# Second FFN by seven block products: the output product by token halves, one half's operands first, four column blocks together

## The chip, the cores and the metric

The kernel runs on one core of one Trainium2 chip. The core has five engines that run side by side and wait for each other by semaphores: TensorE (PE, matrix products into the accumulator memory PSUM), VectorE (DVE), ScalarE (ACT), GpSimd (POOL) and SyncE (SP, which here issues the DMA transfers, one after the other from one queue). The metric is the device time of one execution in microseconds (us), the median over the runs.

## The reference

A decoder trunk of two layers on 1024 tokens of width 1024 in float32. Layer 0 is a Conformer convolution, layer 1 an attention with forget gates; behind each stands an FFN of inner width 4096 and a gated per-layer embedding. The change touches the end of layer 1's attention and layer 1's FFN:

```python
h = h + o @ attn_w_o                       # the attention's output product
hn = rmsnorm(h, ffn_norm[i])               # per token: divided by its root mean square
h = h + jnp.square(jax.nn.relu(hn @ ffn_w1[i])) @ ffn_w2[i]
```

## The kernel before

Activations are kept transposed: features on the 128 partitions, tokens along the free axis, in two halves of 512 tokens (h = 0, 1). A tile hTb0 or hTb1 is one half of the residual, 8 panels of 128 features. A matrix product in the precision wanted takes three matmuls: each operand is split into a high half (a cast to fp32r on ScalarE, line 111) and a low half (the value less its high half, a subtraction on VectorE or GpSimd, line 112), and high by high, low by high and high by low are added in PSUM. Each matmul is 128 x 128 by 128 x 512.

**Attention output product** (`out_product`, L770 to L776; accumulators ps_wo, weights wo). It is done in two parts along the inner dimension: panels 0 to 4 for half 0, then for half 1, then panels 5 to 7 for both halves by turns. Each result is added to hTb on VectorE.

**Operands of the FFN** (`tokens`, L420). For each half the statistics: squares on ScalarE (sq_f), summed on VectorE (acc_f), a small matmul set with a column of 1/1024 (st_f), a mean (ms_f, VectorE), a power of -1/2 (r_f, GpSimd), a broadcast by matmul (bc_f) and its copy (bs_f, ScalarE). f10 is half 0's, f11 half 1's. Then the normed activations, in blocks of 4 panels (z1, z2; L428 is the norm: scale, gain and broadcast in one instruction for a panel), their differences (L439), and of the seven operand blocks the high and low halves (xf).

**The FFN** (`ffn_both`) takes both matrix products by blocks: tokens in two halves, inner features in two halves, columns in two halves, so that seven block products do the work of eight, at the price of sums and differences of blocks. The products are numbered 1 to 7; `seven` runs them in the order 1, 5, 6, 3, 7, 2, 4. Products 1, 6, 7 and 4 accumulate in one bank per output (chain 0), 5, 3 and 2 in another (chain 1). A bank that goes on from one product to the next is first read out. The weight blocks of a product are made in `weight`: for products 5, 6 and 3 the tile t (wt in the first matrix, wu in the second) is built up by a sum or difference on VectorE (L408, L410, L412), for 7 a raw block is overwritten (L414).

- First matrix (`ffn_in`, accumulators psa, raw weights rwa, split weights wa): eight groups of two column blocks, 2 x 12 matmuls per product. Evacuations e, relu and square (L527) and the differences (L532) make the operands of the second matrix's seven products, which go to DRAM (rd).
- Second matrix (`ffn_out`, accumulators psb, rwb and wb): four column groups c of four outputs, 48 matmuls per product. Operands are loaded from DRAM (rb) and split again (rx). The results are added to the residual, which was put by in DRAM (hd) and comes back as hTc0 and hTc1. The raw weights of a group are two tiles of 2 MB; three such buffers exist.

The order on each engine is that in which the program is written, but for statistics, whose matmuls get a higher priority in a scheduling pass; the transfers on SyncE's queue are issued in that order too, each as soon as what it waits for is done.

## Time and profile before

| | us |
|---|---|
| median of 3 runs | 2645.2 |
| lowest and highest | 2643.66, 2648.96 |
| the profiled execution | 2649.79 |
| its span | 2648.1 |
| TensorE busy in the span | 2460.8 |
| VectorE busy | 1794.9 |
| ScalarE busy | 1066.6 |
| GpSimd busy | 938.1 |

The span runs from the first to the last instruction in the trace of one execution; the rest of an execution's time lies around it. TensorE is busy for 93% of it, so what matters is where it is not, and what it waits for there. The slices of the page are 66 us wide; the views below go to the two places by their times.

### The profile page before, as it was taken

The page shows a single profiled execution, that of the slowest core. Times are in us where ns is not written, and L with a number is a line of the kernel's source. Part 1 is how long each engine was busy: PE and PEld are TensorE (multiplying, and loading weights), DVE is VectorE, ACT ScalarE, POOL GpSimd, SP SyncE. Part 2 cuts the span into 40 slices and gives each one's busy share as a digit, 9 for nine tenths or more (in the row PEclk, how much of TensorE's full clock was granted, in tenths as well). Part 3 has the DMA queues.
Part 4 walks back from the last instruction along what each step waited for, and adds up shares of the span by engine and source line. Part 5 has one row for each costly group of instructions (what it writes and reads, how often), then busy time and mean ns, then how long its engine had stood idle before and what let it go on. Part 6 is the DMA issues. An engine that isn't in the chain of part 4 may idle for free.

```text
span 2648.1 us, 31325 instructions
## 1 busy us (share of the span) xinstructions
PE 2460.8 (93%) x11672; PEld 2055.2 (78%) x11672; DVE 1794.9 (68%) x2719; ACT 1066.6 (40%) x1646; POOL 938.1 (35%) x759
## 2 busy tenths in 40 slices
PE   7996899999999999989999999797699995999996
PEld 6885778888888888868888887586588884888875
DVE  7999999525644346565677776756856657777765
ACT  5245433223433225334565665633333233343442
POOL 3464534444000000013666665611632223454400
PEclk9998899999999999989999999898899997999997
DMA  3124123333323333222111111332234455443133
GB/s 130 48 77 170 62 82 98 101 97 96 95 90 101 96 96 100 96 106 68 55 43 54 43 64 57 104 106 93 91 134 157 175 190 208 159 159 127 52 123 112
DMA packets 92008, 272.37 MB, mean 103 GB/s; under 512 B 9280, under 2 KB 14016, under 8 KB 89808
## 3 DMA queue, kind: packets, MB, share of 16 engines
q1 hardware_dynamic: 90704, 266.17, 29.6%
q10 hardware_dynamic: 1152, 4.19, 0.4%
q8 instruction: 92, 1.51, 0.2%
q14 instruction: 60, 0.49, 0.1%
HBM read 216.26 MB, written 54.07 MB: 102 GB/s over the span
## 4 chain that ended last, share of the span: by engine, by line
PE 77%; DVE 13%; ACT 3%; issue 2%; POOL 2%; DMA 2%; SPq 0%; DVEq 0%; POOLq 0%; ACTq 0%
PE ps_fb L137 13%; PE ps_fa L137 12%; PE psb L137 10%; PE psa L137 10%; PE ps_gt L137 6%; PE psq L137 3%; DVE ya L332 3%; PE psv L137 3%; PE psk L137 3%; PE pg L137 3%; PE ps_wo L137 3%; PE pa L137 3%; PE po L946 2%; PE t L976 2%; PE ps_pw L137 2%
## 5 line engine op out<-in xcount | busy, mean ns | idle before, releaser
L137 PE MATMUL psa<-xf,wa 128*128 128x512 f32 x1344 | 315.3, 397 | 21.3 <-ACT wa L111 13.6
L137 PE MATMUL psb<-rx,wb 128*128 128x512 f32 x1344 | 307.7, 391 | 27.2 <-ACT wb L111 26.9
L137 PEld LDWEIGHTS psa<-xf,wa 128*128 128x128 f32 x1344 | 257.7, 192 | 78.5 <-ACT wa L111 14.5
L137 PEld LDWEIGHTS psb<-rx,wb 128*128 128x128 f32 x1344 | 253.8, 189 | 81.2 <-ACT wb L111 27.3
L332 DVE SCALAR_TENSOR_TENSOR ya<-u,wdw,ya 128x512 f32<-128x512 f32 x420 | 284.0, 745 | 0.0
L111 ACT CAST wh_fb<-raw_fb 128x1024 fp32r<-128x1024 f32 x64 | 67.2, 1053 | 213.9 <-PE ps_fb L137 134.7
L111 ACT CAST wh_fa<-raw_fa 128x1024 fp32r<-128x1024 f32 x64 | 67.4, 1053 | 206.4 <-PE ps_fa L137 110.6
L390 DVE TENSOR_TENSOR hT<-ps_fb,hT 128x512 f32<-128x512 f32 x64 | 44.1, 688 | 147.8 <-PE ps_fb L137 147.8
L205 POOL TENSOR_TENSOR r_g<-ms_g,mhalf 128x4 f32<-128x4 f32 x4 | 5.3, 1326 | 375.8 <-DVE ms_g L203 375.8
L928 POOL TENSOR_SCALAR pr<-pr,sm 128x896 f32<-128x896 f32 (+7 forms) x128 | 98.1, 768 | 100.3 <-DVE sm L927 94.1
L112 DVE TENSOR_TENSOR pt<-t,pt 128x512 fp32r<-128x512 f32 (+1 forms) x160 | 99.1, 633 | 49.9 <-ACT pt L111 48.8
L946 PE MATMUL po<-pt,V 128*128 128x256 f32 x640 | 122.2, 307 | 9.5 <-ACT pt L111 7.5
L112 POOL TENSOR_TENSOR wb<-rwb,wb 128x1024 fp32r<-128x1024 f32 x32 | 81.8, 2556 | 122.4 <-ACT wb L111 122.4
L112 DVE TENSOR_TENSOR rx<-rb,rx 128x1024 fp32r<-128x1024 f32 x56 | 92.2, 1654 | 48.6 <-ACT rx L111 48.5
L926 ACT ACTIVATE pr<-pr,sm 128x896 f32<-128x896 f32 (+7 forms) x128 | 99.3, 776 | 51.6 <-DVE sm L925 34.8
L906 POOL TENSOR_SCALAR pr<-cb,ctok 128x896 f32<-128x896 f32 (+7 forms) x128 | 105.4, 829 | 38.9 <-PE t L976 31.2
L920 DVE CUSTOM_DVE_ANT_0 pr<-s,pr 128x512 f32<-128x512 f32 (+2 forms) x192 | 103.4, 550 | 22.5 <-POOL pr L907 11.7
L384 DVE SCALAR_TENSOR_TENSOR fa<-ps_fa,bs_f 128x512 f32<-128x512 f32 x64 | 43.8, 689 | 108.7 <-PE ps_fa L137 105.2
L111 ACT CAST pt<-t 128x512 fp32r<-128x512 f32 (+1 forms) x160 | 83.9, 539 | 76.3 <-PE t L976 73.1
L112 POOL TENSOR_TENSOR wl_fb<-raw_fb,wh_fb 128x1024 fp32r<-128x1024 f32 x32 | 77.3, 2419 | 104.6 <-ACT wh_fb L111 104.6
L112 POOL TENSOR_TENSOR wl_fa<-raw_fa,wh_fa 128x1024 fp32r<-128x1024 f32 x32 | 79.1, 2471 | 91.0 <-ACT wh_fa L111 90.9
L976 PE MATMUL t<-ident,pr 128*128 128x128 f32 x576 | 97.5, 280 | 11.2 <-POOL pr L928 6.0
(355 smaller groups left out, 7043.9 us busy)
## 6 DMA issues: line engine op xcount, KB each, us to landing
raw_fa<-in_wf SPq DMA_DIRECT2D x64, 512.0 KB, 3.4
raw_fb<-in_wf SPq DMA_DIRECT2D x64, 512.0 KB, 3.5
rd<-e SPq DMA_DIRECT2D x112, 256.0 KB, 3.5
rb<-rd SPq DMA_DIRECT2D x28, 1024.0 KB, 5.3
rwa<-in_wf SPq DMA_DIRECT2D x32, 512.0 KB, 5.8
rwb<-in_wf2s SPq DMA_DIRECT2D x8, 2048.0 KB, 9.7
raw_gt<-in_wgate SPq DMA_DIRECT2D x24, 512.0 KB, 3.6
proj<-pj SPq DMA_DIRECT2D x32, 256.0 KB, 2.4
```

The lines of the kernel that those rows point to most:

```text
L111: copy(h, src)
L112: sub.tensor_tensor(l, src, h.bitcast(F32), ALU.subtract)
L137: self.nc.tensor.matmul(ps, p[:, k, :], q[:, k, :], start=(start and k == k0 and n == 0), stop=(stop and k == kt - 1 and n == 2), skip_gro ...
L332: nc.vector.scalar_tensor_tensor(d, s(j), w(j), o, ALU.mult, ALU.add)
L384: nc.vector.scalar_tensor_tensor(t, ps, 0.0, s[h][1], ALU.max, ALU.mult)
L390: nc.vector.tensor_tensor(hT[h][:, j, :], ps, hT[h][:, j, :], ALU.add)
L906: nc.gpsimd.tensor_scalar(z, cb[:, 0:W], -1.0, self.ctok[:, i, n : n + 1], ALU.mult, ALU.add)
L920: nc.vector.tensor_tensor_reduce(zz, ps[:, 0 : hi - lo], zz, -1.0, 3.0e38, ALU.add, ALU.min, sm[:, m : m + 1])
L926: nc.scalar.activation(z, z, AF.Exp, bias=sm[:, 0:1], scale=-1.0, accum_out=sm[:, 2:3])
L928: nc.gpsimd.tensor_scalar(z, z, sm[:, 3:4], 1.0, ALU.mult, ALU.mult)
L946: nc.tensor.matmul(po, V[:, j, n % 4, :], pt[:, q, c : c + 256], start=(j == 0 and q == 0), stop=(jp == u and jj == 1 and q == 1),)
L976: nc.tensor.transpose(ps[:, c : c + P], pr[b][:, j * P : (j + 1) * P], self.ident)
```

## The change

- The attention's output product is done for half 0 to its end (panels 0 to 4, 5 to 7), then for half 1. Behind half 0 stands `tokens_first`: half 0's statistics and the operands 1 and 2, which need half 0 alone. The rest of half 1's product is written behind that.
- `tokens_rest` (half 1's statistics and operands 5, 6, 3, 7, 4) is written behind product 1 and product 2 of the first matrix. The low halves of all operands are subtracted on VectorE, not on GpSimd. Operand 2 is stored to DRAM and loaded again for the later groups (x2b).
- The first call of `ffn_in` takes groups 0 and 1 together: four outputs, 48 matmuls per product. The products run in the order 1, 2, 5, 6, 3, 7, 4 (but in the last column group of the second matrix, which keeps the old order), and product 2 accumulates in a chain of its own.
- Raw weights are tiles of 512 KB, one per block (and pair of outputs), in pools of 4 (wr, used by both matrices) and 8 (wq), loaded one by one; the second matrix's array is laid out anew for that. The blocks of the second matrix's operands are loaded into the place of their low half.
- Product 4's result is put through relu and square on ScalarE.

```diff
-    def tokens(self, hT, gain, name):
-        hd = self.dr.tile([NH, P, KT * HB], F32, name=f"hd_{name}")
-        bc = [self.stats(hT, h, name)[1] for h in range(NH)]
...
-            for q in range(2):
-                s = slice(2 * q, 2 * q + 2)
-                self.split(src[:, s], x[p][:, 0, s], x[p][:, 1, s], sub=nc.gpsimd)
...
+    def parts(self, src, xh, xl, sub=None):
+        for q in range(2):
+            s = slice(2 * q, 2 * q + 2)
+            self.split(src[:, s], xh[:, s], xl[:, s], sub=sub)
+        return xh, xl
+    def tokens_first(self, hT, gain, name):
+        hd = self.dr.tile([NH, P, KT * HB], F32, name=f"hd_{name}")
+        self.nc.sync.dma_start(hd[0], hT[0].rearrange("p k t -> p (k t)"))
+        bc = self.stats(hT, 0, name)[1]
+        f = self.slot([P, 2, 4, HB], F32, f"z0{name}")
+        x = {}
+        for p, i in ((1, 0), (2, 1)):
+            self.norm4(f[:, i], hT[0], gain, 4 * i, bc)
+            t = self.block(f"x{name}{p}")
+            x[p] = self.parts(f[:, i], t[:, 0], t[:, 1])
+        return hT, x, f, hd, gain, name
+    def tokens_rest(self, hT, x, f, hd, gain, name):
+        nc.sync.dma_start(hd[1], hT[1].rearrange("p k t -> p (k t)"))
+        xd = self.dr.tile([P, 2, 4, HB], F32, name=f"xd_{name}")
+        bc = self.stats(hT, 1, name)[1]
+        g = self.slot([P, 2, 4, HB], F32, f"z1{name}")
...
+        def later():
+            nc.sync.dma_start(xd[:, 0], x[2][0].bitcast(F32))
+            nc.sync.dma_start(xd[:, 1], x[2][1].bitcast(F32))
+            self.norm4(g[:, 1], hT[1], gain, 4, bc)
+            self.diff(f[:, 0], g[:, 1], f[:, 0])
+            new(6, f[:, 0])
+            new(3, g[:, 1])
+            self.diff(g[:, 0], g[:, 1], g[:, 0])
+            self.diff(f[:, 1], f[:, 1], f[:, 0])
+            new(7, g[:, 0])
+            new(4, f[:, 1])
+            t = self.block(f"x{name}2b")
+            nc.sync.dma_start(t.bitcast(F32), xd)
+            x[2] = (t[:, 0], t[:, 1])
+        self.norm4(g[:, 0], hT[1], gain, 0, bc)
+        self.diff(f[:, 0], g[:, 0], f[:, 0])
+        new(5, f[:, 0])
+        return later
-    def seven(self, w, x, n, k4, name, banks, done):
+    def seven(self, w, x, n, k4, name, done, order=(1, 2, 5, 6, 3, 7, 4), between=None):
-        for p in (1, 5, 6, 3, 7, 2, 4):
+        for p in order:
-            chain = {1: 0, 6: 0, 7: 0, 4: 0, 5: 1, 3: 1, 2: 1}[p]
+            chain = {1: 0, 6: 0, 7: 0, 4: 0, 5: 1, 3: 1, 2: 2}[p]
...
+            if between:
+                between(p)
...
-                for g in range(8):
...
-                    self.ffn_in(l, g, raw, sp, x, rd)
+                load(0)
+                load(1)
+                rest = []
+                def between(p):
+                    if p == 1:
+                        rest.append(self.tokens_rest(*first))
+                    elif p == 2:
+                        rest[0]()
+                self.ffn_in(l, (0, 1), raw, sp, x, rd, between)
+                for g in range(2, 8):
+                    load(g)
+                    self.ffn_in(l, (g,), raw, sp, x, rd)
...
-                wr = self.pool(c2, f"wq{l}", 3)
+                wq = self.pool(c2, f"wq{l}", 8)
...
-            if p == 4:
                 o = tt(p)
-                nc.scalar.copy(o, ps)
-                square(o, o)
-                keep(2, i, o)
...
+                nc.scalar.activation(o, ps, AF.Relu)
+                nc.scalar.activation(o, o, AF.Square)
+                keep(2, o)
...
+        for b in range(4):
+            for q in range(2):
+                pool, tag = (wq, "wq") if b > 1 else (wr, "wr")
+                raw = pool.tile([P, 2, HB], F32, name=f"rwb{l}{c}{b}{q}", tag=tag)
+                nc.sync.dma_start(raw, self.a["wf2s"][l, c, q, :, b].rearrange("p (n f) -> p n f", n=2))
+                raws[q].append(raw)
...
+        order = (1, 5, 6, 3, 7, 2, 4) if c == 3 else (1, 2, 5, 6, 3, 7, 4)
+        self.seven(w, x, 4, 4, f"b{l}{c}", done, order)
...
-            for h in range(NH):
-                for _ in self.out_product(0, KSPLIT, (h,), self.at):
+            for k0, k1, h in ((0, KSPLIT, 0), (KSPLIT, NP, 0), (0, KSPLIT, 1)):
+                for _ in self.out_product(k0, k1, (h,), self.at):
...
+            first = self.tokens_first(self.hn, "ffn1", "f1")
+            for _ in self.out_product(KSPLIT, NP, (1,)):
                 pass
-        return self.hn
+        return first
```

TensorE at joint 1, between the output product and the products of the first matrix. psa10_ij names group 0's accumulators: the first of the three digits is the chain, the second the product that began it, the third the output; xf1p is the operand of product p, wa10p and wa11p are the weights of groups 0 and 1. Before:

```order
L137 MATMUL ps_wo571_15059<-xoh1_13676,wl_wo570_15045 128x512
L189 MATMUL st_f10_15088<-meanm_75,acc_f10_15089 128x1 x4
L158 MATMUL bc_f10_15120<-ident_68,r_f10_15118 128x128 x4
L189 MATMUL st_f11_15127<-meanm_75,acc_f11_15128 128x1 x4
L158 MATMUL bc_f11_15159<-ident_68,r_f11_15157 128x128 x4
L137 MATMUL psa10_010_15235<-xf11_15171,wa101_15236 128x512 x12
L137 MATMUL psa10_011_15253<-xf11_15171,wa101_15236 128x512 x12
L137 MATMUL psa10_150_15268<-xf15_15182,wa105_15270 128x512
```

Both sets of statistics stand ahead of the first product. In the changed kernel:

```order
L137 MATMUL psa10_012_15243<-xf11_15028,wa111_15244 128x512 x10
L137 MATMUL psa10_013_15261<-xf11_15028,wa111_15244 128x512 x10
L189 MATMUL st_f11_15278<-meanm_75,acc_f11_15279 128x1 x4
L158 MATMUL bc_f11_15310<-ident_68,r_f11_15308 128x128 x4
L137 MATMUL psa10_220_15329<-xf12_15037,wa102_15330 128x512 x12
L137 MATMUL psa10_221_15348<-xf12_15037,wa102_15330 128x512 x12
L137 MATMUL psa10_222_15364<-xf12_15037,wa112_15365 128x512 x12
L137 MATMUL psa10_223_15383<-xf12_15037,wa112_15365 128x512 x12
L137 MATMUL psa10_150_15433<-xf15_15324,wa105_15435 128x512
L137 MATMUL psa10_151_15452<-xf15_15324,wa105_15435 128x512
```

Half 0's statistics have gone from here (they stand among the matmuls of the output product), and half 1's stand between product 1 (operand xf11) and product 2 (xf12), which now has two pairs of outputs.

VectorE at the same place in the changed kernel, from the last sums of half 1's squares (acc_f11) to the low half of the operand of product 5 (xf15); wt10 is group 0's weight sum, e101 and e111 are results of products 1 and 2:

```order
L197 TENSOR_TENSOR acc_f11_15279<-acc_f11_15279,sq_f11_6_15296 128x512
L197 TENSOR_TENSOR acc_f11_15279<-acc_f11_15279,sq_f11_7_15299 128x512
L409 TENSOR_TENSOR wt10_15208<-wt10_15208,rwa100_15195 128x1024
L203 TENSOR_SCALAR ms_f11_15306<-st_f11_15278 128x4
L422 SCALAR_TENSOR_TENSOR z1f1_15317<-hTb1_13907,vec_66,bs_f11_15315 128x512 x8
L436 TENSOR_TENSOR z0f1_15023<-z1f1_15317,z0f1_15023 128x1024 x2
L582 TENSOR_TENSOR e101_15226<-psa10_220_15329,e101_15226 128x512
L582 TENSOR_TENSOR e111_15241<-psa10_221_15348,e111_15241 128x512
L436 TENSOR_TENSOR z1f1_15317<-z1f1_15317 128x1024 x2
L583 SCALAR_TENSOR_TENSOR e101_15226<-e101_15226 128x512
L112 TENSOR_TENSOR xf15_15324<-z0f1_15023,xf15_15324 128x1024
```

The mean of half 1 (ms_f11) stands behind the next difference of weights (wt10), and eight norms, four instructions of differences and three on product 2's results stand between it and xf15.

SyncE's queue at joint 2, where the second matrix's weights (rwb) are loaded. rb10p and rx10p are the loads of its operand p for the column group 0, rd the stores of the first matrix's results, the last two digits of rwb10bq the block b and the pair of outputs q. Before:

```order
L580 DMA rb102_17689<-rd1_15074 128x4x512
L524 DMA rd1_15074<-e1714_17326 128x512
L524 DMA rd1_15074<-e1718_17330 128x512
L568 DMA rwb100_17342<-in_wf2s 128x4096
L568 DMA rwb101_17345<-in_wf2s 128x4096
L568 DMA rwb110_17823<-in_wf2s 128x4096
L580 DMA rb104_17758<-rd1_15074 128x4x512
L580 DMA rb111_17829<-rd1_15074 128x4x512
```

The first load of weights stands behind the last stores of the first matrix. In the changed kernel the blocks 0 and 1 stand some thirty places further ahead, and here stand the blocks 2 and 3:

```order
L634 DMA rx107_17762<-rd1_15182 128x4x512
L579 DMA rd1_15182<-e11410_17376 128x512
L579 DMA rd1_15182<-e1154_17391 128x512
L579 DMA rd1_15182<-e11510_17395 128x512
L634 DMA rx104_17828<-rd1_15182 128x4x512
L622 DMA rwb1020_17410<-in_wf2s 128x1024
L622 DMA rwb1021_17412<-in_wf2s 128x1024
L622 DMA rwb1030_17414<-in_wf2s 128x1024
L622 DMA rwb1031_17416<-in_wf2s 128x1024
L622 DMA rwb1120_17900<-in_wf2s 128x1024
```

They follow the load of operand 4 (rx104), whose memory is free when product 1 of the second matrix is done.

## Rows read from the trace of the kernel before

**Rows 1.** The span and the mean granted clock of the core.
```profile
core 0: 2648.1 us, clock 0.961
```
**Rows 2.** TensorE's timeline: start, us, instructions, [idle before, releaser]; last row up to 2230.
```profile
1822.94 0.39 PE L137 MATMUL ps_wo<-xoh,wl_wo 128*128 128x512 f32 x1
1823.46 1.05 PE L189 MATMUL st_f<-meanm,acc_f 128*128 128x1 f32 x8
...
1840.07 1.86 PE L189 MATMUL st_f<-meanm,acc_f 128*128 128x1 f32 x8 [10.07 <-DVE acc_f L197]
1845.78 2.08 PE L158 MATMUL bc_f<-ident,r_f 128*128 128x128 f32 x8 [3.85 <-POOL r_f L205]
1847.51 8.10 PE L137 MATMUL psa<-xf,wa 128*128 128x512 f32 x26
...
1916.58 267.51 PE L137 MATMUL psa<-xf,wa 128*128 128x512 f32 x1172 [0.36 <-POOL wa L112]
2210.97 2.08 PE L137 MATMUL psb<-rx,wb 128*128 128x512 f32 x4 [26.88 <-ACT wb L111]
2213.41 305.67 PE L137 MATMUL psb<-rx,wb 128*128 128x512 f32 x1340 [0.36 <-POOL wb L112]
...
2213.41 16.89 PE L137 MATMUL psb<-rx,wb 128*128 128x512 f32 x66 [0.36 <-POOL wb L112]
```
**Rows 3.** Windows: stretch, us, each engine's busy us, granted clock, DMA share, GB/s.
```profile
1823.50:1847.40 23.90, 6.57 (x31) 6.11 (x32) 20.85 (x20) 8.94 (x13) 12.52 (x5) 0.59 0.38 161
1847.40:1916.60 69.20, 47.89 (x176) 36.73 (x174) 55.38 (x44) 21.46 (x26) 44.79 (x16) 0.82 0.19 67
1916.60:2184.00 267.40, 267.40 (x1172) 221.06 (x1172) 163.36 (x200) 82.15 (x106) 70.47 (x27) 0.99 0.46 166
2184.00:2211.00 27.00, 0.12 (x2) 0.03 (x1) 12.60 (x14) 7.99 (x9) 0.01 (x1) 0.54 0.87 320
```
**Rows 4.** The chain that ended last, across joint 2: start, us, what.
```profile
2199.24 10.61 DMA rwb<-in_wf2s
...
2210.99 2.37 POOL wb L112
```
**Rows 5.** ScalarE's timeline at joint 1.
```profile
1823.11 3.21 ACT L174 ACTIVATE sq_f<-hTb 128x512 f32<-128x512 f32 x6
1826.22 1.03 ACT L111 CAST wa<-rwa 128x1024 fp32r<-128x1024 f32 x1
...
1847.89 0.58 ACT L211 COPY bs_f<-bc_f 128x512 f32<-128x512 f32 x1 [10.15 <-PE bc_f L158]
```
**Rows 6.** VectorE's timeline at joint 1.
```profile
1832.80 2.73 DVE L428 SCALAR_TENSOR_TENSOR z1f<-hTb,vec,bs_f 128x512 f32<-128x512 f32 x4
...
1851.17 2.35 DVE L439 TENSOR_TENSOR z1f<-z1f 128x1024 f32<-128x1024 f32 x2
1853.44 6.99 DVE L428 SCALAR_TENSOR_TENSOR z2f<-hTb,vec,bs_f 128x512 f32<-128x512 f32 x4
...
1874.92 9.06 DVE L428 SCALAR_TENSOR_TENSOR z2f<-hTb,vec,bs_f 128x512 f32<-128x512 f32 x4
...
1891.02 0.69 DVE L547 TENSOR_TENSOR e<-psa,e 128x512 f32<-128x512 f32 x1 [4.77 <-ACT e L535]
```
**Rows 7.** GpSimd's timeline at joint 1.
```profile
1825.94 1.93 POOL L205 TENSOR_TENSOR r_f<-ms_f,mhalf 128x4 f32<-128x4 f32 x1 [68.70 <-DVE ms_f L203]
1827.85 2.74 POOL L112 TENSOR_TENSOR wa<-rwa,wa 128x1024 fp32r<-128x1024 f32 x1
...
1844.71 1.01 POOL L205 TENSOR_TENSOR r_f<-ms_f,mhalf 128x4 f32<-128x4 f32 x1 [2.50 <-DVE ms_f L203]
1854.09 5.79 POOL L112 TENSOR_TENSOR xf<-z1f,xf 128x1024 fp32r<-128x1024 f32 x2 [8.36 <-ACT xf L111]
```
**Rows 8.** Issues of transfers over the span: name, count, KB each, median us to landing.
```profile
rwa<-in_wf SPq DMA_DIRECT2D x32, 512.0 KB, 5.8
rwb<-in_wf2s SPq DMA_DIRECT2D x8, 2048.0 KB, 9.7
```

More of the change, by code (lines that the diff above doesn't have):

```diff
@@ L394, in ffn, with weight @@
             self.linear(a["wf2"][l, c], KT, r, evac2, f"fb{tag}{c}", **kw)
-    def weight(self, raw, t, p, name, pool, sub):
+    def weight(self, A, t, p, name, pool, sub):
         nc = self.nc
-        A = [raw[:, :, b, :] for b in range(4)]
         src = {1: A[0], 2: A[1], 4: A[3], 7: A[2]}.get(p, t)
@@ L466, in seven, with norm4, diff @@
-    def seven(self, w, x, n, k4, name, banks, done):
+    def norm4(self, dst, src, gain, k0, bc):
+        for k in range(4):
+            self.nc.vector.scalar_tensor_tensor(
+                dst[:, k], src[:, k0 + k, :], self.v(gain, k0 + k), bc, ALU.mult, ALU.mult
+            )
+    def parts(self, src, xh, xl, sub=None):
[3 more added lines that the diff above has]
+        return xh, xl
+    def diff(self, d, a, b):
+        for q in range(2):
+            s = slice(2 * q, 2 * q + 2)
+            self.nc.vector.tensor_tensor(d[:, s], a[:, s], b[:, s], ALU.subtract)
@@ L476, in seven, with ffn_both @@
                 ps = bank[chain, i]
-                self.mm3(ps, w(p, i), (xp[:, 0], xp[:, 1]), k4, start=first, more=not first)
+                self.mm3(ps, w(p, i), xp, k4, start=first, more=not first)
                 done(p, i, ps)
-    def ffn_both(self, hT, l):
+            if between:
+                between(p)
+    def ffn_both(self, l, first):
         nc, a = self.nc, self.a
@@ L489, in ffn_both @@
             sp = self.pool(c, f"sw{l}", 2)
+            wr = self.pool(c, f"wr{l}", 4)
+            hT, x, _, hd, gain, name = first
             with ExitStack() as c1:
                 self.tt = self.pool(c1, f"ev{l}", 16)
[L492 to L503 removed]
@@ new lines, in w, with keep, add @@
+            if i % 2 == 0:
+                sub = nc.vector if p in ((1, 2) if between else (5, 6, 7)) else nc.gpsimd
+                ws[p, g] = self.weight(raw[g], t[g], p, f"a{l}{g}{p}", sp, sub)
+            return ws[p, g][i % 2]
+        def done(p, i, ps):
+            d, k = c[i], 2 * gs[0] + i
+            tt = lambda q: self.tmp(f"e{l}{k}{q}")
+            ve = nc.vector.tensor_tensor
+            def keep(q, t):
+                nc.sync.dma_start(rd[q, k], t)
+            def add(o):
+                ve(o, ps, o, ALU.add)
+                nc.vector.scalar_tensor_tensor(o, o, 0.0, o, ALU.max, ALU.mult)
+                return o
@@ new lines, in ffn_in, with ffn_out @@
+        self.seven(w, lambda p: x[p], 2 * len(gs), 4, f"a{l}{gs[0]}", done, between=between)
+    def ffn_out(self, l, c, hT, load_h, wr, wq, sp, rd):
+        nc = self.nc
+        raws, ts, ws = [[], []], [], {}
+        for b in range(4):
+            for q in range(2):
+                pool, tag = (wq, "wq") if b > 1 else (wr, "wr")
+                raw = pool.tile([P, 2, HB], F32, name=f"rwb{l}{c}{b}{q}", tag=tag)
+                nc.sync.dma_start(raw, self.a["wf2s"][l, c, q, :, b].rearrange("p (n f) -> p n f", n=2))
+                raws[q].append(raw)
+        ts = [sp.tile([P, 2, HB], F32, name=f"wu{l}{c}{q}", tag="t") for q in range(2)]
```

161 lines of the change are left out of this document (60 added, 101 removed).

## The prediction

> **What bounds the kernel now.** I read the whole span first, then a table by stretch, then TensorE's own timeline, and only then the other engines at two places. The span is 2648.1 us at a mean granted clock of 0.961 [rows 1]; the profiled execution took 2649.79 us, 4.6 us above the median of the runs (2645.2), so I make the sum on the profiled one and move it over by the difference. The reader should see in TensorE's timeline [rows 2] that the second FFN is two long blocks without a gap, 1172 matmuls in 267.51 us and 1340 in 305.67 us (0.228 us each), and that all it loses lies at two joints. **Joint 1** runs from the end of the attention output product (1822.94 + 0.39 = 1823.3) until TensorE runs freely at 1916.6. **Joint 2** is the 26.88 us between the first matrix (its last matmul ends at 1916.58 + 267.51 = 2184.1) and the second. In both stretches TensorE is also granted less clock, 0.59 and 0.82 at joint 1 and 0.54 at joint 2 [rows 3], so that the first matmuls after a gap are slow: 26 of them took 8.10 us, 0.31 each, about 2.2 us more than at full pitch [rows 2].
>
> What each joint costs: the first matrix has 1344 matmuls; at 0.2283 us they are 306.8 us, and the stretch from 1823.3 to 2184.1 is 360.8, so joint 1 costs **54.0 us**. At joint 2 the gap is 26.9, the next wait 0.4, and the first 70 matmuls lose about 2.8 at the lower clock: **30.1 us**. Everything else that the change touches runs beside a TensorE that does not stop. So only the joints are worth counting, and the gain cannot pass 84 us.
>
> What ends the waits: at joint 1 VectorE. It is busy 20.85 of 23.9 us and 55.38 of 69.2 [rows 3]; it makes the sums of half 1, all normed blocks and all differences, and TensorE waits 10.07 us for acc_f and later for operands and weights [rows 2]. At joint 2 it is the transfer of the second matrix's weights: the first 2 MB load takes 10.61 us, issued only at 2199.24, since the queue of SyncE holds it behind loads and stores of the first matrix's results; then a cast and a GpSimd subtraction of 2.37 follow before the low part can be used [rows 4].
>
> **The change, part by part. Joint 1.** Times are on the clock of before, which holds up to the output product.
>
> (a) Output product: the same 384 matmuls, but half 0 is complete first, and the statistics of half 0 (a matmul set on the mean, 1.05, and a broadcast, 2.08 in the rows [rows 2]) now stand inside it instead of behind it. On ScalarE three squares of half 0 (0.535 each: 3.21 for six [rows 5]) stand ahead of the first cast of half 1's last panels; I count 2.2 us for that wait and 1.6 for what the small matmuls add. It ends at 1827.1, 3.8 late.
>
> (b) Product 1, now over four outputs (48 matmuls, 11.0 us). The broadcast's copy is there at 1825.5 (0.58 [rows 5]). Then VectorE does eight norms (2.73 for four, so 5.4 with their overlap [rows 6]), one last addition (0.69 [rows 6]) of the output product, and a sum of two weight blocks, the low half of the weights and the first low half of the operand (1.17 each, half of 2.35 for two alike [rows 6]). That is 1835.2. TensorE idled, so it pays 2.2 of low clock: product 1 ends at 1847.4.
>
> (c) The statistics of half 1. Their squares stand behind the copies of product 1's results on ScalarE: 0.3 for the last copy, eight squares and sums of 0.535, the last addition on VectorE at about 1853. The mean on VectorE stands behind a difference of weights (wt10) that waits for a subtraction on GpSimd: a cast 1.03 [rows 5] and 2.74 [rows 7] after the squares, so about 1857. The power on GpSimd takes 1.01 to 1.93 [rows 7], the broadcast 2.08: 1860.4. In TensorE's queue both small sets stand ahead of product 2, so product 2 waits for them although its operands are ready; that is 13 us of idle time. Product 2: 11.0 + 2.1 at low clock, to 1873.5.
>
> (d) Product 5 needs the new operand: copy 0.6, eight norms 5.4, two differences 2.3, two additions of product 2's results 1.3, two more differences 2.3, a square 0.65, a low half 1.2: 13.7 us after 1860.4, if VectorE is alone. It isn't: GpSimd subtracts weights for 5.5 us at that time, and four norms that take 2.73 alone took 6.99 while GpSimd subtracted [rows 6, 7]. 5.5 us at that pace do 2.1 us of work, so I add 3.4: product 5 starts in earnest at about 1877.9 and ends at 1890.4 (46 matmuls 10.5, low clock 2).
>
> (e) From there 1200 matmuls are left, 274.0 us, and I allow 1 us for product 6's low half. End of the first matrix: 2165.4 instead of 2184.1. Joint 1 then costs 2165.4 - 1823.3 - 306.8 = 35.3, **a gain of 18.7 us**. Bounds: if every wait of (c) and (d) took as long as today's, nothing; if TensorE waited only for product 1's first operand (about 12 us with the 3.8 of (a)) and three low clocks (6), 36.
>
> [...]
>
> **Joint 2.** The weights' first two blocks now fit in buffers that come free during the last group, so the loads for products 1 and 2 are issued some 40 us before the end of the first matrix, and product 1 of the second matrix is interleaved with the last product of the first. What is late next is the other two blocks, for product 5. Their loads stand in SyncE's queue behind the load for product 4, which waits for the end of product 1. Counted from the start of the last group's product 7, that end is 96 matmuls or 21.9 us; then 1 MB and the weights have to pass (3 MB with both halves of both blocks). At the 320 GB/s of the stretch [rows 3] that is 9.4 to 10 us, a landing at 32; by the median landings, 5.8 us for 512 KB and 9.7 for 2 MB [rows 8], it is 28 (one block alone) to 37 (1 MB taken as half of 9.7, then 2 MB). TensorE wants product 5 at 144 matmuls, 32.9. A sum on VectorE (1.2), a cast (1.0) and a subtraction on GpSimd (2.4) come between: the low half at 36.6 to 37.3, and TensorE, after 6 matmuls that need only the high half, stops for about 3 us, and for about 4.5 in all with the other pair of outputs, whose weights come a cast and a subtraction later. Adding 1.5 for low clock and 1 for the interleaved start, joint 2 costs 7.0: **a gain of 23.1 us**. Bounds: 28 if the blocks land before they are wanted; 12 if they land as late as the three loads of before (10.61 from issue, one behind the other) and the clock drops.
>
> **At no cost:** the relu and square on ScalarE instead of VectorE (ScalarE busy 82 of 267 us there [rows 3]); the weight blocks in 2 KB and 4 KB rows (queues 0.46 busy [rows 3]); operand 2 written out and loaded again (3 MB under product 6, wanted 50 us later). The results of half 1 go out in the same number of stores. If that cover is gone, each costs about its landing, 5 us, once.
>
> Sum: 2649.8 - 18.7 - 23.1 = 2608.0 for an execution like the profiled one; 2645.2 - 41.8 = **2603.4 us** for the median.
>
> **Rivals.**
> B. Joint 1 gains next to nothing: VectorE is at the contended pace through all of step (d), 13.1 us times 6.99/2.73 = 33.5, 17 more than the 13.1 + 3.4 counted, and 1.7 of joint 1's gain is left. For: every four norms while GpSimd works took 6.99 or 9.06 [rows 6]. Against: the operands' low halves leave GpSimd (its 5.79 us beside the 6.99 were two of them [rows 7]), and only the weights' stay. Gain 25: 2620 us.
> C. Both joints close nearly: the statistics of half 1 run beside product 1, product 2 follows at once, and the late blocks land in time. Joint 1 then costs the 12 us up to product 1 and some 8 for low clock and product 5's operand, joint 2 costs 2: gain 34 + 28, 2583. Against it stands the order on TensorE's queue.
> D. Slower. Product 7 now stands directly in front of product 4, and both add into the same bank, so that product 4's first matmul waits for VectorE to have read product 7's result. The slack is the other output, 12 matmuls or 2.7 us (before, product 2 stood between: 8.2 us), in six groups. VectorE is busy 163 of 267 us [rows 3] and the read takes 0.69 [rows 6]; if work queued ahead of it made it late by 2.7 + 7 us in each group, six times 7 us would eat the 42. At 9 us more in each group it would be 2657. Against it: from 1916.6 on VectorE is idle for 104 of 267 us [rows 3], and eight pieces of 1.17 [rows 6] would have to stand ahead of the read in every group.
> E. It does not do what it says: the early loads are held behind stores of the last group and nothing else moves; 2640 to 2650.
>
> **How the numbers follow.** Forecast (2592 to 2614) 0.50; B 0.20; C 0.14; D 0.07; E and mixtures 0.09, of which 0.05 still faster. A change within 0.2% (5.3 us) could not be told from none: faster 0.89, same 0.04, slower 0.07. The range must reach C below and B above with some 5 us for the unknowns of the loads: 2580 to 2626, which leaves out part of C, D and E.
>
> **What would show it.** Step (a): the output product ends 3 to 5 us later. (b, c): product 1 runs from about 1830 to 1847, then TensorE is idle some 13 us and its wait ends with the broadcast. (d): product 5 done near 1890; near 1907 it is B, near 1875 C. Joint 2: product 1 of the second matrix without a gap, and a wait of 2 to 6 us ahead of product 5, ended by GpSimd's or ScalarE's part of the weights. A wait at each group's product 4 ended by VectorE would be D. I would be wrong above all if (c) is not the wait that I think, since it carries half of joint 1.

## The result and the profile after

The changed kernel takes 2613.97 us (median of four runs, 2610.33 to 2616.24), the kernel before beside it 2644.89 (2643.66 to 2648.96): a ratio of 0.9879, interval 0.9862 to 0.9896, or 30.9 us less. The profiled execution took 2616.24 us, its span is 2614.5 us at a mean clock of 0.969 (against [rows 1]).

One reading rule comes first. The two traces run the same work up to the output product of the attention, and yet do not reach it at the same time. TensorE's timeline of the kernel before, and then of the changed one, at the first matmul of the output product (start, us, instructions, [idle before, releaser]):

```profile
1725.99 0.50 PE L137 MATMUL ps_wo<-xoh,wh_wo 128*128 128x512 f32 x1 [0.29 <-ACT wh_wo L111]
```
```profile
1722.14 0.50 PE L137 MATMUL ps_wo<-xoh,wh_wo 128*128 128x512 f32 x1 [0.17 <-ACT wh_wo L111]
```

Over all traces of this study that point lies between 1719.70 and 1725.99 us, and in two kernels that are the same up to joint 2 it is 1722.14 and 1725.36. So 3.85 of the 33.6 us between the two spans came by chance ahead of the change, and I count from this matmul, T0, in every run. What is left, 29.8 us, is near the 30.9 of the medians.

TensorE's timeline of the changed kernel, joints 1 to 3:

```profile
1804.73 0.50 PE L137 MATMUL ps_wo<-xoh,wh_wo 128*128 128x512 f32 x1 [2.16 <-ACT wh_wo L111]
...
1824.57 0.39 PE L137 MATMUL ps_wo<-xoh,wl_wo 128*128 128x512 f32 x1
...
1832.97 12.06 PE L137 MATMUL psa<-xf,wa 128*128 128x512 f32 x44 [0.76 <-DVE xf L112]
1854.21 1.87 PE L189 MATMUL st_f<-meanm,acc_f 128*128 128x1 f32 x8 [9.17 <-DVE acc_f L197]
1857.42 2.08 PE L158 MATMUL bc_f<-ident,r_f 128*128 128x128 f32 x8 [1.34 <-POOL r_f L205]
1859.15 12.36 PE L137 MATMUL psa<-xf,wa 128*128 128x512 f32 x50
1876.23 17.12 PE L137 MATMUL psa<-xf,wa 128*128 128x512 f32 x64 [4.72 <-DVE xf L112]
1896.19 34.30 PE L137 MATMUL psa<-xf,wa 128*128 128x512 f32 x150 [2.85 <-POOL wa L112]
1931.52 2.99 PE L137 MATMUL psa<-xf,wa 128*128 128x512 f32 x12 [1.03 <-DVE e L582]
1936.03 8.46 PE L137 MATMUL psa<-xf,wa 128*128 128x512 f32 x36 [1.53 <-DVE e L582]
...
2169.00 2.88 PE L137 MATMUL psa<-xf,wa 128*128 128x512 f32 x12
2171.72 18.97 PE L137 MATMUL psb<-rx,wb 128*128 128x512 f32 x82
2196.39 285.84 PE L137 MATMUL psb<-rx,wb 128*128 128x512 f32 x1248 [5.70 <-ACT wb L111]
```

It answers to [rows 2]. Product 1 now runs from 1833 (before, from 1847.5), product 2 from 1859, but product 5 starts in earnest only at 1876.2, and after that four waits of over 1 us are left (2.85, 1.03, 1.53 and, ahead of the second matrix's product 5, 5.70) where before there were 26.88 us at joint 2 alone. The table by stretch, beside [rows 3] (us, busy us of PE, PEld, DVE, ACT, POOL, granted clock, DMA share, GB/s):

```profile
1823.50:1847.40 23.90, 15.48 (x55) 11.19 (x53) 20.46 (x23) 11.86 (x16) 0.00 (x0) 0.85 0.42 176
1847.40:1896.00 48.60, 33.08 (x130) 27.01 (x130) 41.22 (x43) 19.72 (x25) 17.59 (x5) 0.79 0.13 43
1944.30:2162.00 217.70, 217.46 (x959) 179.83 (x958) 140.40 (x151) 75.77 (x99) 58.45 (x23) 1.00 0.50 177
2171.80:2196.40 24.60, 18.90 (x84) 15.07 (x82) 20.85 (x23) 9.94 (x11) 6.13 (x2) 0.98 0.90 326
```

At joint 1 VectorE is still the busy engine, 20.46 of 23.9 us and 41.22 of 48.6; at joint 2 TensorE keeps a clock of 0.98 (before 0.54).

From the rows come three sums. The first matrix ends at 2169.00 + 2.88, less 14 matmuls of the second matrix that run among its own (3.2 us): 2168.7, or 446.5 after T0; before it was 2184.1, 458.1 after T0. **Joint 1 gained 11.6 us.** From there to the end of the second matrix it takes 313.5 us (to 2196.39 + 285.84 = 2482.2), before 335.0: **joint 2 gained 21.5.** And from the end of the second matrix to the end of the span it takes 132.3 us, before 129.0 (2648.1 less 2213.41 + 305.67): **a third joint, ahead of the gate, lost 3.3.**

The same three columns, worked out in this way from the rows of every run below, which the experiments draw on (us; the first matrix of e7, e12 and before has no matmuls of the second among its own):

```
run        T0       first matrix   second matrix   rest of   median of
                    ends, from T0  from there      the span  the runs
before     1725.99  458.1          335.0           129.0     2644.9
after      1722.14  446.5          313.5           132.3     2614.0
e1         1723.00  444.8          312.1           132.2     2613.3
e2         1723.16  435.4          311.8           131.9     2603.9
e3         1720.57  438.4          313.1           132.1     2607.5
e4         1722.18  452.2          312.6           131.7     2621.7
e5         1722.70  448.9          311.6           132.1     2616.2
e6         1719.70  445.8          311.7           132.2     2611.7
e7         1722.80  443.9          327.4           127.9     2622.5
e8         1725.36  444.3          311.4           131.7     2615.4
e9         1725.50  446.9          312.2           131.9     2616.4
e10        1724.02  446.8          311.5           127.5     2610.2
e11        1724.60  433.0          311.9           127.6     2599.5
e12        1722.99  446.2          335.8           129.1     2629.9
```

After, e7, e8 and e10 are one kernel up to joint 2, but for transfers, and give 443.9 to 446.8: a difference of 3 us in that column shows nothing; nor does one of 2 in the next, and I take the median of a single kernel as good to some 3 us, an estimate from the 5.9 us over which the four runs of the changed kernel spread.

### The profile page after: what moved, and what is told of

It is laid out like the page before. It is cut to its first block, busy times and chain, and to the rows that moved or that the text cites. A ratio compares the mean times of both kernels' runs of the same rounds, so it can differ in the third digit from the quotient of the medians.

```text
span 2614.5 us, 31465 instructions
## 1 busy us (share of the span) xinstructions
PE 2457.6 (94%) x11672; PEld 2053.1 (79%) x11672; DVE 1778.6 (68%) x2723; ACT 1078.3 (41%) x1670; POOL 913.1 (35%) x747
## 3 DMA queue, kind: packets, MB, share of 16 engines
q1 hardware_dynamic: 99840, 271.94, 30.1%
## 4 chain that ended last, share of the span: by engine, by line
PE 76%; DVE 14%; issue 3%; ACT 3%; POOL 2%; DMA 2%; DVEq 0%; SPq 0%; POOLq 0%; ACTq 0%
PE ps_fb L137 13%; PE ps_fa L137 12%; PE psb L137 9%; PE psa L137 8%; PE ps_gt L137 7%; PE ps_wo L137 3%; PE psq L137 3%; DVE ya L332 3%; PE psv L137 3%; PE pg L137 3%; PE psk L137 3%; PE pa L137 3%; PE po L1002 2%; PE t L1032 2%; PE ps_pw L137 2%
## 5 line engine op out<-in xcount | busy, mean ns | idle before, releaser
L137 PE MATMUL psa<-xf,wa 128*128 128x512 f32 x1200 | 281.4, 396 | 16.8 <-DVE xf L112 5.5
L137 PEld LDWEIGHTS psa<-xf,wa 128*128 128x128 f32 x1200 | 228.4, 191 | 68.2 <-DVE xf L112 6.6
L112 DVE TENSOR_TENSOR pt<-t,pt 128x512 fp32r<-128x512 f32 (+1 forms) x160 | 99.2, 634 | 48.6 <-ACT pt L111 47.5
L112 POOL TENSOR_TENSOR wb<-rwb,wb 128x1024 fp32r<-128x1024 f32 x32 | 87.2, 2734 | 95.9 <-ACT wb L111 86.6
L112 DVE TENSOR_TENSOR rx<-rx 128x1024 fp32r<-128x1024 f32 x56 | 79.9, 1437 | 41.8 <-ACT rx L111 41.8
L1002 PEld LDWEIGHTS po<-pt,V 128*128 128x128 f32 x640 | 92.8, 196 | 18.7 <-ACT pt L111 12.4
```

What stands on the lines that cost most here:

```text
L112: sub.tensor_tensor(l, src, h.bitcast(F32), ALU.subtract)
L137: self.nc.tensor.matmul(ps, p[:, k, :], q[:, k, :], start=(start and k == k0 and n == 0), stop=(stop and k == kt - 1 and n == 2), skip_gro ...
L1002: nc.tensor.matmul(po, V[:, j, n % 4, :], pt[:, q, c : c + 256], start=(j == 0 and q == 0), stop=(jp == u and jj == 1 and q == 1),)
```

## The experiments

**Joint 1: what does product 5 wait for?** The prediction's theory was TensorE's queue: half 1's small matmul sets stand ahead of product 2 and hold it up. The rival was VectorE's chain: sums of squares, mean, eight norms, differences, low half of operand 5. e1 writes half 1's statistics and operands behind product 2, so that the queue holds nothing up; e2 goes the other way and writes the statistics ahead of product 1; e3 writes only the squares and sums there. e1:

```diff
-                    if p == 1:
-                        rest.append(self.tokens_rest(*first))
-                    elif p == 2:
-                        rest[0]()
+                    if p == 2:
+                        self.tokens_rest(*first)()
```

e2, in front of the first matrix and in `tokens_rest`:

```diff
+                bc = self.stats(hT, 1, name)[1]
...
-        bc = self.stats(hT, 1, name)[1]
```

e3, in the same two places (`sums` is the squares and sums cut out of the statistics; the rest has their usual priority, not the raised one):

```diff
+                acc = self.sums(lambda k: hT[1][:, k, :], f"{name}1")
...
-        bc = self.stats(hT, 1, name)[1]
+        bc = self.stats(hT, 1, name, 1, acc)[1]
```

> Half 1's statistics are written behind product 2 instead of product 1, so that product 2 does not stand behind them on TensorE. Theory A (VectorE's chain from half 1's sums to the low half of operand 5 sets when product 5 can start, and TensorE's order only moves the gap): product 2 follows product 1 without the 13 us gap, the gap moves ahead of product 5, and the time is that of the changed kernel (2614 us) within 4 us. Theory B (the order on TensorE's queue costs the gap, as step (c) of the prediction put it): 9 to 12 us faster, about 2603.

> Half 1's statistics are written ahead of product 1. Theory A: the norms of half 1 start some 15 us sooner; product 1 waits for the broadcast until about 1843, but from there products 1, 2 and 5 run through: 8 to 12 us faster than the changed kernel, 2602 to 2606. Theory B: what product 1 loses eats what product 2 gains, 2610 to 2616.

> Only the squares and sums of half 1 are written ahead of product 1; the mean, power and broadcast stay behind it without raised priority. Theory A: product 1 runs as in the changed kernel, the gap of 13 us ahead of product 2 goes, and product 5's operand is ready some 14 us sooner: 11 to 16 us faster, 2598 to 2603. Theory B: the same gap goes, 9 to 12 us faster; the two are told apart by e1.

e1 takes 2613.28 us (0.988, 0.9865 to 0.9895 against before). Its TensorE timeline:

```profile
1831.86 24.57 PE L137 MATMUL psa<-xf,wa 128*128 128x512 f32 x94 [3.22 <-ACT wa L111]
1861.62 1.76 PE L189 MATMUL st_f<-meanm,acc_f 128*128 128x1 f32 x8 [5.20 <-DVE acc_f L197]
1868.18 2.07 PE L158 MATMUL bc_f<-ident,r_f 128*128 128x128 f32 x8 [4.79 <-POOL r_f L205]
1878.57 2.07 PE L137 MATMUL psa<-xf,wa 128*128 128x512 f32 x4 [8.31 <-ACT xf L111]
1880.90 49.27 PE L137 MATMUL psa<-xf,wa 128*128 128x512 f32 x212 [0.26 <-DVE xf L112]
```

Products 1 and 2 run through in 24.57 us, and the time is the same: the idle time only moved behind them, and product 5 starts 155.6 us after T0, where the changed kernel has 154.1. Freeing the queue brings nothing by itself. It is not a test of the queue alone, though: VectorE now takes product 2's results among half 1's sums and ahead of its mean, so that the broadcast starts 9.9 us later after T0 (145.2 against 135.3), and its work up to product 5 is only put in another order. e2 takes 2603.94 us (0.9843, 0.9829 to 0.9858), 10.0 less than the changed kernel, all of it in the first column of the table:

```profile
1838.61 1.87 PE L189 MATMUL st_f<-meanm,acc_f 128*128 128x1 f32 x8 [12.64 <-DVE acc_f L197]
1845.28 2.07 PE L158 MATMUL bc_f<-ident,r_f 128*128 128x128 f32 x8 [4.80 <-POOL r_f L205]
1847.01 25.32 PE L137 MATMUL psa<-xf,wa 128*128 128x512 f32 x108
1872.71 3.96 PE L137 MATMUL psa<-xf,wa 128*128 128x512 f32 x16 [0.38 <-DVE e L582]
```

From T0, TensorE starts product 1 thirteen us later than in the changed kernel and ends the first matrix eleven sooner: products 1 and 2 now cover VectorE's norms and differences, and product 5 follows at once, with a wait of 0.38 and, further on, one of 2.24 us inside it. In both kernels VectorE's chain starts with half 1's sums; the broadcast comes 122.1 us after T0 in e2, 135.3 in the changed kernel and 119.8 in the kernel before. So the change, which starts TensorE early, starts VectorE's chain 15 us late. e3 gains 6.5 (2607.5; 0.9863, 0.9846 to 0.9879), less than both theories expected. Its broadcast starts 124.1 us after T0, almost as early as e2's, but product 5 then waits in pieces of 1.3 to 2.6 us for ScalarE and VectorE; why, no run separates.

**Joint 1: the two other parts of its rebuilding.** e6 takes group 0 alone in the first call, e9 puts the output product back into its old order, and half 0's operands behind it (they still come ahead of half 1's).

```diff
-                self.ffn_in(l, (0, 1), raw, sp, x, rd, between)
-                for g in range(2, 8):
+                self.ffn_in(l, (0,), raw, sp, x, rd, between)
+                for g in range(1, 8):
```
```diff
-            for k0, k1, h in ((0, KSPLIT, 0), (KSPLIT, NP, 0), (0, KSPLIT, 1)):
-                for _ in self.out_product(k0, k1, (h,), self.at):
+            for h in range(NH):
+                for _ in self.out_product(0, KSPLIT, (h,), self.at):
...
-            first = self.tokens_first(self.hn, "ffn1", "f1")
-            for _ in self.out_product(KSPLIT, NP, (1,)):
+            for _ in self.out_product(KSPLIT, NP):
                 pass
+            first = self.tokens_first(self.hn, "ffn1", "f1")
```

> The first call takes group 0 alone, so products 1 and 2 are 24 matmuls each instead of 48. The cover ahead of product 5 falls by 11 us, while half 1's squares, which stand behind product 1's copies, come 5.5 us sooner, and the operands 6, 3, 7 and 4 are wanted at twice the pace: 5 to 12 us slower than the changed kernel, 2619 to 2626. Rival (the cover is of no use, since VectorE's chain starts when product 1 ends): 5 us faster, 2609.

> Alone undone against the changed kernel: the output product goes back to its old order (panels 0 to 4 for half 0, for half 1, then 5 to 7 for both halves by turns), and half 0's statistics and operands are written behind it. Theory A (the time of joint 1 is set by what stands in VectorE's one chain of work, and half 0's part of it can start early only if half 0 is complete early): TensorE loses the cover of half 1's last panels, 5 to 8 us of it, product 1 starts 5 to 8 us later counted from the end of the output product, and all behind it shifts: 2619 to 2622 us. Rival: the order of the output product buys nothing by itself, since its own wait of 2.2 us goes away and the chain from half 1's sums to operand 5 is what product 5 waits for: 2611 to 2616 us.

e6: 2611.67 us (0.9881, 0.9865 to 0.9896), e9: 2616.35 (0.9888, 0.987 to 0.9906); both end the first matrix where the changed kernel does (445.8 and 446.9 against 446.5). Neither the four column blocks nor the output product by halves, each undone alone, brings anything that can be told from chance; by the medians too both stay within 2.4 us of the changed kernel. For e6 neither expectation came true, for e9 the rival did. In e9 the output product ends 6 us sooner after T0 (96.8 against 102.8), product 1 starts in earnest 2.2 us sooner, and the sums of half 1 come 2.0 us sooner; what half 0's completeness buys, the product's own wait of 2.16 us and the small matmuls pay.

**Joint 1: the low halves.** e4 puts the low halves of operands 5, 6, 3, 7 and 4 back on GpSimd; e12 does the opposite to the kernel before, and nothing else: the low halves of all seven operands go to VectorE.

```diff
-            x[p] = self.parts(src, t[:, 0], t[:, 1])
+            x[p] = self.parts(src, t[:, 0], t[:, 1], self.nc.gpsimd)
```
```diff
-                self.split(src[:, s], x[p][:, 0, s], x[p][:, 1, s], sub=nc.gpsimd)
+                self.split(src[:, s], x[p][:, 0, s], x[p][:, 1, s])
```

> The low halves of operands 5, 6, 3, 7 and 4 are subtracted on GpSimd again, as before the change. [...] Rival (GpSimd's weights are what waits: one subtraction took 7.9 us beside VectorE's low halves): no slower, 2610 to 2614.

> The kernel before with one part of the change alone: the low halves of all seven operands of the FFN at joint 1 are subtracted on VectorE and not on GpSimd. Nothing else is moved; half 0 and half 1 are still made together and product 5 still follows product 1. Theory: the move is a gain of its own, since VectorE's four norms at 6.99 and 9.06 us fall towards 2.73 when GpSimd doesn't subtract beside them, which is worth more than the 14 low halves of 1.2 us that VectorE takes on: 3 to 8 us faster than the kernel before, 2637 to 2642 us. Rival: VectorE's chain only gets longer by what the norms win, and the gain of joint 1 comes from starting on one half's operands: 2643 to 2650 us.

e4 loses 7.7 us (2621.66; 0.9912, 0.9897 to 0.9927), so its rival is out. e12 is the surprise: 2629.89 us, 0.9934 (0.9921 to 0.9947), 16.5 less than the kernel before, twice what the theory allowed. Even its profiled execution, the slowest of its six, ends the first matrix 446.2 us after T0: where the changed kernel does. That is 11.9 of the 16.5; the trace does not place the rest. VectorE's timeline in e12, at the place of [rows 6], and GpSimd's:

```profile
1852.01 2.73 DVE L428 SCALAR_TENSOR_TENSOR z2f<-hTb,vec,bs_f 128x512 f32<-128x512 f32 x4
1854.66 2.35 DVE L112 TENSOR_TENSOR xf<-z1f,xf 128x1024 fp32r<-128x1024 f32 x2
...
1861.47 3.49 DVE L112 TENSOR_TENSOR xf<-z2f,xf 128x1024 fp32r<-128x1024 f32 x3
...
1867.14 3.49 DVE L428 SCALAR_TENSOR_TENSOR z2f<-hTb,vec,bs_f 128x512 f32<-128x512 f32 x2
```
```profile
1854.68 14.75 POOL L112 TENSOR_TENSOR wa<-wt,wa 128x1024 fp32r<-128x1024 f32 x1 [10.39 <-ACT wa L111]
```

The four norms that took 6.99 us take 2.73, a low half takes 1.2 where GpSimd took 2.9 [rows 7], and the other four norms, 9.06 before, take 4.9 (3.49 and 1.40). So one line of the change, put into the kernel before, gives all that joint 1 gave. The other way round, e4 keeps the rebuilding and ends the first matrix at 452.2, 5.9 us sooner than before: the rebuilding (with the low halves of operands 1 and 2 alone on VectorE) gives 5.9, the move 11.9, both together 11.6. They do not add up.

**Joint 1: the tail.** TensorE's wait of 2.85 us for GpSimd belongs to the low half of product 6's weights. The list of the change does not have it, but in the first call the change also exchanges who subtracts the low halves of weights: those of products 1 and 2 stand on VectorE and those of 5, 6 and 7 on GpSimd, where the kernel before had it the other way round. e5 puts product 6's on VectorE in the first call.

```diff
-                sub = nc.vector if p in ((1, 2) if between else (5, 6, 7)) else nc.gpsimd
+                sub = nc.vector if p in ((1, 2, 6) if between else (5, 6, 7)) else nc.gpsimd
```

> The low halves of product 6's weights in the first call (two subtractions) go from GpSimd to VectorE. If the subtraction that took 7.9 us on GpSimd beside VectorE's low halves is what TensorE waited 2.85 us for, that wait goes and 2.4 us of work join VectorE's chain: 0 to 3 us faster than the changed kernel, 2611 to 2614. Rival (VectorE's chain is late by all that is added to it): 2 us slower, 2616.

2616.22 us (0.9894, 0.9879 to 0.9908), no gain; the first column is 2.4 us longer, which is within chance. The wait did not go, it moved to the next subtraction that GpSimd still has, product 3's: the order on TensorE is not wholly the written one, and 24 matmuls of product 3 stand ahead of the last ones of product 6. TensorE in e5:

```profile
1891.81 1.19 PE L137 MATMUL psa<-xf,wa 128*128 128x512 f32 x4 [0.69 <-ACT wa L111]
1900.33 35.92 PE L137 MATMUL psa<-xf,wa 128*128 128x512 f32 x146 [7.33 <-POOL wa L112]
```

**Joint 2.** e7 exchanges the two pools of raw weights, so that blocks 0 and 1 are no longer loaded early. e8 takes operand 4's load, behind which the prediction saw the late blocks, out of SyncE's queue.

```diff
-                pool, tag = (wq, "wq") if b > 1 else (wr, "wr")
+                pool, tag = (wr, "wr") if b > 1 else (wq, "wq")
```
```diff
-            nc.sync.dma_start(o[:, 1].bitcast(F32), rd[p, 4 * c : 4 * c + 4].rearrange("k p t -> p k t"))
+            (nc.scalar if (c, p) == (0, 4) else nc.sync).dma_start(o[:, 1].bitcast(F32), rd[p, 4 * c : 4 * c + 4].rearrange("k p t -> p k t"))
```

> The pools of the second matrix's raw weights change places: the blocks 2 and 3 get the memory that comes free during the last group, the blocks 0 and 1 the memory that comes free with its end. So the loads for products 1 and 2 are late as before the change, those for product 5 early. If joint 2's gain is the early loads: 17 to 22 us slower than the changed kernel, 2631 to 2636. Rival (smaller loads and the interleaving do most of it): 5 to 10 us slower, 2619 to 2624.

> Operand 4 of the second matrix's first column group is loaded from ScalarE's queue, so that the loads of the blocks 2 and 3 no longer stand behind it on SyncE's. If that place is what makes product 5 wait, as the prediction says: the wait of 5.7 us falls to 2 or less, 2610. Rival (the stores of the last results ahead of both, and operand 4's split ahead of the weight sum on VectorE, set the time): the loads are issued 2 us sooner at most and the wait stays 4 to 5.7, 2612 to 2614.

e7: 2622.51 us (0.9916, 0.9901 to 0.9931), 8.5 more than the changed kernel. By that the rival would be right; but the exchange of pools also gives back 4.4 us at the end (see joint 3). At joint 2 TensorE waits once, 18.02 us, and the second column of the table grows by 13.9; so 13.9 of joint 2's 21.5 us are the early loads of blocks 0 and 1, net of product 5's wait, which is gone in e7 since blocks 2 and 3 are early there. For the other 7.6 the chain of e7 points to the smaller tiles, though half of the group's bytes are early in e7 as well: its first load, issued late again, is on the way for 3.76 us, where the 2 MB of before took 10.61 [rows 4]. A run with large tiles loaded early was not made. TensorE, and the chain that its wait ends:

```profile
2184.67 149.80 PE L137 MATMUL psb<-rx,wb 128*128 128x512 f32 x648 [18.02 <-ACT wb L111]
```
```profile
2172.06 7.71 DMA rd<-e
...
2179.79 3.76 DMA rwb<-in_wf2s
...
2183.57 1.05 ACT wb L111
```

e8: 2615.43 us (0.9889, 0.9873 to 0.9906), and a wait of 4.50 us ahead of product 5 where the changed kernel had 5.70. That is no gain: kernels that share the changed kernel's joint 2 show 4.17 to 5.81. The chain of the changed kernel, and SyncE's queue in the changed kernel and in e8, tell why:

```profile
2181.85 0.32 SPq L579
...
2182.26 7.09 DMA rx<-rd
...
2189.43 1.06 ACT rx L111
...
2192.34 0.89 DVE rx L112
...
2194.07 1.14 DVE wu L407
...
2195.29 1.05 ACT wb L111
```
```profile
2184.03 5.67 SPq L622 DMA_DIRECT2D rwb<-in_wf2s  x8
```
```profile
2177.71 5.40 SPq L579 DMA_DIRECT2D rd<-e  x3
2185.38 4.08 SPq L622 DMA_DIRECT2D rwb<-in_wf2s  x8
```

In both the last stores of the first matrix's results (rd) leave near 2182 to 2183, and all stands behind them; with operand 4's load out of the way the weights are issued at 2185.4 instead of 2184.0. Counted from the end of the first matrix that is 15.7 us for 15.3, no sooner. In the changed kernel the chain runs through operand 4's own load and split (rx), behind which VectorE's sum of weights (wu) stands; in e8 that sum waits 0.18 us for the weights instead. So two paths of nearly the same length begin at those stores, and taking one away brings nothing. That the stores set the wait is read from the chains; no run moves them.

**Joint 3.** e10 exchanges the pools in the last column group alone, e11 does that and e2's edit together.

```diff
-                pool, tag = (wq, "wq") if b > 1 else (wr, "wr")
+                pool, tag = (wq, "wq") if (b > 1) != (c == 3) else (wr, "wr")
```

> The changed kernel with the two pools of the second matrix's raw weights exchanged in the last column group alone. It moves nothing at joints 1 and 2; at the end of the second matrix it puts the last additions on the residual ahead of the last sums of squares on VectorE, as in the kernel before. Theory: the 3.2 us that the time from the second matrix's end to the end of the span has grown come from that order; they come back: 2610 to 2611 us, and that time falls from 132 to 128 or 129 us. Rival: they come from something else there (the relu and square on ScalarE, the smaller loads); 2613 to 2616 us and 132 us.

> Both edits that the runs point to: half 1's statistics written ahead of the first matrix, and the two pools exchanged in the last column group alone. If the two places are independent, the gains of 10 and 3 to 4 us add up: 2599 to 2601 us. If the third joint's order is not what costs there, 2604 us as with the statistics alone.

VectorE at the end of the second matrix, in the changed kernel (TensorE ends at 2482.2) and in e10 (2482.4), the last additions on the residual (L643):

```profile
2484.33 0.69 DVE L643 TENSOR_TENSOR hTc<-psb,hTc 128x512 f32<-128x512 f32 x1
2485.81 0.75 DVE L231 SCALAR_TENSOR_TENSOR g1xl<-hTc,vec,g1xh 128x512 fp32r<-128x512 f32 x1 [0.79 <-ACT g1xh L230]
2486.47 0.69 DVE L643 TENSOR_TENSOR hTc<-psb,hTc 128x512 f32<-128x512 f32 x1
```
```profile
2483.21 0.74 DVE L231 SCALAR_TENSOR_TENSOR g1xl<-hTc,vec,g1xh 128x512 fp32r<-128x512 f32 x1
2483.87 0.68 DVE L643 TENSOR_TENSOR hTc<-psb,hTc 128x512 f32<-128x512 f32 x1
```

The last addition starts 4.2 us after TensorE's end in the one and 1.5 in the other; in between VectorE waits 0.79 us at a time for ScalarE. e10 takes 2610.23 us (0.9867, 0.9852 to 0.9882), and its rest of the span 127.5 us: the loss goes with that order. e11, at 2599.47 us (0.9826, 0.9812 to 0.9841), is the fastest kernel of the study, 14.5 us under the changed one, and the two gains add up as expected.

## Why the prediction came out as it did

The time was in the range, 2614.0 for 2603.4, at the upper end of the forecast's own band (2592 to 2614), and 41.8 us of gain were 29.8 to 30.9. The missing 12 us lie in three places, and one reason was wrong though its number stood.

**Steps (a) to (d): the times held.** On before's clock (3.85 us later) the output product ends at 1828.8 (predicted 1827.1; its wait was 2.16 for 2.2), product 1 at 1848.9 (1847.4), product 2 starts at 1863.0 (1860.4), product 5 at 1880.1 (1877.9). That is 2.2 us late in all, 1.7 of them from (a). The 3.4 us that (d) adds for GpSimd's subtractions show in two places of VectorE's chain: two differences in 3.37 us where two others took 2.35, and a low half in 3.36 where the next took 1.21, together 3.2; both times GpSimd subtracted weights beside them, from 1866.84 for 3.25 us and from 1872.28 for 2.82. Some of the working has slips that moved little: the terms of (b) add up to 1848.4, not 1847.4, those of (d) to 1877.5, not 1877.9; and operand 2 goes out and back as 4 MB, not 3. Rival B, the contended pace through the whole step, is out, with eight norms in 5.39 us:

```profile
1860.15 5.39 DVE L422 SCALAR_TENSOR_TENSOR z1f<-hTb,vec,bs_f 128x512 f32<-128x512 f32 x8 [3.88 <-ACT bs_f L211]
1865.46 2.35 DVE L436 TENSOR_TENSOR z0f<-z1f,z0f 128x1024 f32<-128x1024 f32 x2
...
1868.93 3.37 DVE L436 TENSOR_TENSOR z1f<-z1f 128x1024 f32<-128x1024 f32 x2
...
1872.82 3.36 DVE L112 TENSOR_TENSOR xf<-z0f,xf 128x1024 fp32r<-128x1024 f32 x1
```

**Step (c): the wait is there, but joint 1 does not hang on it.** "In TensorE's queue both small sets stand ahead of product 2, so product 2 waits": it does, 14.1 us, but e1 takes the sets away and gains nothing, since VectorE's chain still comes as late to product 5. So the wait did not carry half of joint 1: e9 and e6 each undo a part of what was rebuilt around it at no loss, and e12 reaches the same end with products and halves in the old order. All that joint 1 gave can be had from the low halves' move off GpSimd alone, which the prediction names only in an argument against rival B. That its sum came out near for joint 1 up to product 5 is no proof of (c): the sum follows VectorE's chain all the way. The early products 1 and 2 are real cover, but the change pays for them with half 1's sums, 15 us later; e2 pays less and gets 10 us more.

**Step (e): the 1 us allowance was mis-sized.** Product 5's last 46 matmuls take 13.04 us from 1876.23 and end at 1889.3, on before's clock 2.7 us later than predicted. From there the first matrix took 279.4 us, 4.4 longer than predicted: waits of 2.85, 1.03 and 1.53 us stand there. The first is product 6's low half, as named; GpSimd needed 10.23 us for two subtractions beside VectorE's low halves, 7.89 of them for that one:

```profile
1872.28 2.82 POOL L112 TENSOR_TENSOR wa<-wt,wa 128x1024 fp32r<-128x1024 f32 x1 [2.20 <-ACT wa L111]
1888.25 10.23 POOL L112 TENSOR_TENSOR wa<-wt,wa 128x1024 fp32r<-128x1024 f32 x2 [13.16 <-DVE xf L112]
```

The other two are rival D's read of a bank, ended by VectorE. It came at the group pair, where VectorE works without a gap on the results of four outputs; in the six single groups only two waits, of 0.24 and 0.35 us, are left of it. The 2.7 and the 4.4 make joint 1's 11.6 of 18.7.

**Joint 2: the size held, half of the reason did not.** Its cost after is 313.5 less 1344 matmuls at 0.2281 us [rows 2], 7.0 us as predicted; by the same measure before's is 28.4, not 30.1, which is the difference to 23.1. That the 7.0 matches is in part luck: the wait ahead of product 5 was 5.70 for 4.5, and what else joint 2 costs is 1.3 for 2.5. And the place behind operand 4's load, which the prediction gave as the reason, is worth nothing (e8).

**Joint 3 was not in the sum.** "Everything else that the change touches runs beside a TensorE that does not stop" fails at the end of the second matrix: which pool the last group's weights come from changed the order of VectorE's queue there: 3.3 us lost, of which e10 has all back. Rivals C and E did not happen.

## What to carry to other kernels

Where two engines slow each other (here the same four norms took 6.99 us beside GpSimd's subtractions in the kernel before, and 2.73 in e12 with GpSimd idle), work that is moved from one to the other is priced on both, and tried alone before anything is rebuilt around it: here one line gave as much as the whole rebuilding of a joint. Starting the matrix engine early is worth only what the next wait's own chain does not lose by it, so write first what starts the longest chain behind the joint. Look for the change's effect at every place that shares its pools, and count two traces from the last instruction ahead of the change that they have in common: the upstream part alone moved them by up to 6.3 us (T0 from 1719.70 to 1725.99).

## What was not expected of the hardware

In a single instruction GpSimd lost more than VectorE. Beside a VectorE that worked without a gap, one subtraction of 128 x 1024 on GpSimd took 14.75 us in e12, and one 7.89 in the changed kernel (VectorE's work ended 2.2 us ahead of it), where GpSimd's next took 2.39; VectorE's own instructions of that size were at worst 3.4 at joint 1 of the changed kernel instead of 1.21. The 14.75 us lasted through eleven VectorE instructions that followed each other without a gap. In the kernel before VectorE lost more in one place: its four norms took 9.06 us [rows 6], where four took 2.73 with GpSimd idle, and GpSimd's three subtractions beside them 3.38, 2.82 and 2.78:

```profile
1873.87 3.38 POOL L112 TENSOR_TENSOR xf<-z1f,xf 128x1024 fp32r<-128x1024 f32 x1
1877.21 2.82 POOL L112 TENSOR_TENSOR xf<-z2f,xf 128x1024 fp32r<-128x1024 f32 x1
1879.99 2.78 POOL L112 TENSOR_TENSOR xf<-z1f,xf 128x1024 fp32r<-128x1024 f32 x1
```

What decides which of the two is slowed, the runs do not show. It was not tried by itself.
